# Router logits from the raw residual sums instead of the normalised rows, in a one-core hybrid decoder layer

## The chip, the cores and the metric

The kernel runs as one program on one core of a Trainium2 chip. The metric is the device time of one execution in microseconds (us). Three runs of the kernel before gave 1267.33, 1271.27 and 1271.88 us, median 1271.27 us. The engines of the core are TensorE (PE for its matmuls, PEld for the loads of its stationary operand), VectorE (DVE), ScalarE (ACT), GpSimd (POOL) and SyncE (SP), which issues most of the transfers.

## The reference

One layer of a decoder over 512 rows of 1024 channels. What matters here is the end of the first half and the router of the second half:

```python
def _layer_norm(x, eps=1e-5):
    mu = jnp.mean(xf, axis=-1, keepdims=True)
    var = jnp.mean(jnp.square(xf - mu), axis=-1, keepdims=True)
    return ((xf - mu) * lax.rsqrt(var + eps)).astype(x.dtype)

        y = (1 + g1[:, None]) * (merged @ w_out[l])
        x = _layer_norm(ALPHA * x + y) * ln1_g[l] + ln1_b[l]
        h = _layer_norm(x) * (1 + sc2[:, None]) + sh2[:, None]
        y = (1 + g2[:, None]) * _hier_moe(h, router_grp_w[l], router_grp_b[l], ...)

    # in _hier_moe: 4 groups of 8 experts, one group, two experts inside it
    grp_prob = jax.nn.softmax((x @ w_grp + b_grp).astype(jnp.float32), axis=-1)
    grp_p, grp_idx = lax.top_k(grp_prob, 1)
    exp_logits = (x @ w_exp + b_exp).astype(jnp.float32).reshape(NT, N_GROUPS, EXP_PER_GROUP)
    in_grp = exp_logits[jnp.arange(NT), grp_idx[:, 0]]
    top_l, top_i = lax.top_k(in_grp, TOPK_IN_GROUP)
    comb = grp_p * jax.nn.softmax(top_l, axis=-1)
    # then every expert computes (silu(xb @ w1[e]) * (xb @ w3[e])) @ w2[e] on its rows
```

Each row therefore passes two layer norms in a row (the first with gain and bias `ln1_g`, `ln1_b`) before 36 router logits (4 groups, 32 experts) are taken from it.

## The kernel before

The 512 rows are four tiles (i = 0 to 3) of 128 rows. Three stages matter here.

**The output product.** For each tile, `out_piece` computes `merged @ w_out` as 96 matmuls into `pyo` (128x256 each, three terms of a split into high and low parts), and VectorE adds the residual (`z`, L1105) and gathers statistics (`bn_stats`, L1106). Tiles 0 to 2 are evicted in two pieces of 512 columns, tile 3 in four of 256.

**Norms and routing, the generator `ln`.** For each tile: both norms on VectorE and ScalarE (L1156, L1160, L1161, with the two reciprocal roots on ScalarE, L234 and L235), the normalised rows `xh` (ScalarE L1169, for tile 3 VectorE L1167), eight transposes on TensorE (`ph`, L188) with copies to `h2T`, the split of `xh` into `xhh` (ScalarE L1188) and `xhl` (GpSimd L1189), `acc` (ScalarE L1193), the logits `plg` with the router weights stationary, a copy `lgT` and a second small product that turns them back to rows, then the choice of group and experts on VectorE (L1209 to L1224), a matmul `prk` that counts the rows ahead of each row, and the positions and the one-hot matrix `pm` (L1233 to L1242). At the very end `gather_first` multiplies `xhh` and `xhl` by `pm` (`pgx`, 16 matmuls for a tile), which gathers the rows for the first two experts into `xe`.

**The experts.** All 32 experts' weights (512 KB tiles `ew`, 128x1024) stream from memory over SP's queue through a ring of 36 buffers `Q`, which `z`, `xh`, `acc` and the rest share. The first matmuls of this stage are `p` (L184). SP issues in program order: a transfer whose buffer isn't free holds back everything behind it.

**What sets the order.** The program has one order for each engine, fixed when it is built. A class `Weave` carries a modelled clock, advanced by every matmul (`mm`, `tr`); a generator that yields a number is continued when that clock has moved by so many ns. The constants `LN_D1`, `LN_D2` (the yields of `ln`), and the hand-written calls of `W.upto`, `W.drain` and `gather_first` after the loop over tiles, decide where the norm and routing steps of a tile stand among the products of the next one. On the chip each engine works through its own list in order and waits on semaphores.

Of the kernel before, what the change touches and what calls it, by code (L numbers as in the profile page):

```python
# [67 lines left out]
LN_D1, LN_D2 = 9000, 4500  # L68
# [5 lines left out]
GK = 5  # L74
# [67 lines left out]
def hybrid_kernel(ctx, tc, a, out, dbg=None, stop=None):  # L142
# [836 lines left out]
    sel36 = cp.tile([128, 36], F32, name="sel36")  # L979
    V.tensor_add(sel36, ident[:, 0:36], ident[:, 64:100])  # L980
    l1g = l1b = wr = bfs = None

    def prep():
        nonlocal g1b, l1g, l1b, wr, bfs
# [31 lines left out]
        mm(pbr_[:, 0:36], ones, wsh[:, 288:324], True, True)  # L1016
        V.tensor_add(br, br, pbr_[:, 0:36])
# [106 lines left out]
    gp8, gm, em = rtv[:, 0], rtv[:, 1], rtv[:, 2]  # L1124
    V.memset(gp8, -3e38)
# [4 lines left out]
    lg = pk2[:, 256:384].rearrange("p (i n) -> p i n", i=NT)  # L1130
# [9 lines left out]
    pgx0, stage = [], {i: 0 for i in range(NT)}  # L1140

    def gather_first(tiles, ks=range(8)):


        if not pgx0:
            pgx0.extend(PS("pgx").rearrange("p (k s) -> p k s", k=2) for _ in range(4))
        for k in ks:
            for i in tiles:
                for j, x in enumerate((xhh, xhl)):
                    mm(pgx0[k // 2][:, k % 2, :], x[i][:, k * 128:(k + 1) * 128], hots0[i // 2][:, i % 2, :],  # L1150
                       i == 0 and j == 0 and k % 2 == 0, i == NT - 1 and j == 1 and k % 2 == 1)

    def ln(i, z, st):
        last = i == NT - 1
        mv, rs = layer_stats(z, "l1", st, later=True)
        V.scalar_tensor_tensor(z, z, mv[:, 0:1], l1g, op0=OP.subtract, op1=OP.mult)  # L1156
        st = small("l2st", 12)
        for half in range(2):
            s_ = slice(half * 512, (half + 1) * 512)
            V.scalar_tensor_tensor(z[:, s_], z[:, s_], rs[:, 0:1], l1b[:, s_], op0=OP.mult, op1=OP.add)  # L1160
            V.bn_stats(st[:, half * 6:(half + 1) * 6], z[:, s_])  # L1161
        mv, rs = layer_stats(z, "l2", st, later=last)
        xh = Q("xh")
# [6 lines left out]
        probe(f"x1{i}", z)  # L1170
        probe(f"xh{i}", xh)
        stage[i] = 1
        yield LN_D1
        h2 = []
        for k4 in range(2):
            pt = PS("ph2")
            for k in range(4):
                kk_ = k4 * 4 + k
                tr(pt[:, k * 128:(k + 1) * 128], xh[:, kk_ * 128:(kk_ + 1) * 128], ident)
            t = S("h2T")  # L1180
            if last and k4:
                V.tensor_copy(t, pt)
            else:
                A.activation(t, pt, AF.Copy)
            h2.append(t)
# [17 lines left out]
        lgT = S("lgT")[:, 0:128]
        A.activation(lgT, plg[:, 128:256], AF.Copy)
        stage[i] = 2.5
        yield 700
        mm(plg[:, 0:36], lgT, sel36, True, True)

        V.tensor_add(gp8[:, i, 0:4], plg[:, 0:4], br[:, 0:4])  # L1209
# [362 lines left out]
    for n, u in enumerate(units):  # L1572
# [162 lines left out]
```

## Time and profile before

| quantity | value |
|---|---|
| median of three runs | 1271.27 us (1267.33 to 1271.88) |
| the profiled execution | 1271.63 us, its span 1269.9 us |
| granted TensorE clock, mean of the span | 0.977 of full |
| PE busy | 1176.9 us, 93% of the span |
| DVE busy | 701.2 us, 55% |
| ACT busy | 423.6 us, 33% |
| POOL busy | 121.7 us, 10% |
| moved by SP's transfers (q1) | 268.57 MB |

The profile is one execution. Busy shares are means over stages with different limits, so they don't say what the change is worth; the timeline of each engine around the change does, with the idle time in front of an instruction and what ended it. In a timeline row the first number is the start in us from the start of the span, the second the duration; consecutive instructions of the same kind are joined with a count, and brackets hold the idle time before. PE durations include the pipeline, so the pace of a row of matmuls is the distance between their starts.

### The profile page before, as it was taken

What the parts mean: (1) busy time and instruction counts of PE and PEld (TensorE: products, weight loads), DVE (VectorE), ACT (ScalarE), POOL (GpSimd) and SP (SyncE); (2) the same over time, 40 slices, a digit from 0 to 9 for tenths busy, and PEclk for the clock granted to TensorE, in tenths of its full rate; (3) what the DMA queues carried; (4) which work ended last, traced back from release to release, by engine and by line L of the source; (5) the groups of instructions that cost most, each with busy time, mean ns of one, the idle gap of its engine ahead of it and who ended that gap; (6) DMA issues with size and microseconds to landing.
All of it is one profiled execution on the core that took longest, in us unless ns stands there. A gap on an engine that the chain in (4) does not pass through costs nothing. (4 is left out here: it accounts for less than half of the span.)

```text
span 1269.9 us, 18562 instructions
## 1 busy us (share of the span) xinstructions
PE 1176.9 (93%) x6647; PEld 816.0 (64%) x6647; DVE 701.2 (55%) x1629; ACT 423.6 (33%) x897; POOL 121.7 (10%) x179
## 2 busy tenths in 40 slices
PE   5999999999999999999989969999999899889992
PEld 4788898778888888878778964434435235125352
DVE  5564988777566665323586787535135144133446
ACT  5233666664435364555231321201102002002023
POOL 3011111101101011001150140000000000000002
PEclk9999999999999999999998979999999999999996
DMA  9954413324334243335325197999999999999981
GB/s 325 296 150 141 117 54 118 94 94 133 97 117 120 74 158 108 100 114 183 110 98 183 42 339 295 409 408 409 409 409 409 409 410 406 409 409 407 406 324 67
DMA packets 140862, 297.14 MB, mean 234 GB/s; under 512 B 11099, under 2 KB 82979, under 8 KB 140768
## 3 DMA queue, kind: packets, MB, share of 16 engines
q1 hardware_dynamic: 131296, 268.57, 57.6%
q0 software_dynamic: 8704, 25.00, 6.1%
q10 hardware_dynamic: 768, 2.37, 0.5%
q8 instruction: 53, 0.87, 0.3%
q14 instruction: 41, 0.34, 0.1%
HBM read 293.76 MB, written 4.76 MB: 235 GB/s over the span
## 5 line engine op out<-in xcount | busy, mean ns | idle before, releaser
L184 PE MATMUL p<-ew,xe 128*32 128x512 f32 (+1 forms) x960 | 202.6, 598 | 13.1 <-DMA ew<-in_exp_w_dram 12.7
L277 DVE TENSOR_TENSOR wl<-wst,wh 128x1024 fp32r<-128x1024 f32 (+1 forms) x93 | 119.5, 1314 | 74.7 <-ACT wh L276 74.0
L184 PEld LDWEIGHTS p<-ew,xe 128*32 128x32 f32 (+1 forms) x960 | 53.6, 122 | 155.5 <-issue 81.2
L1473 DVE TENSOR_TENSOR s<-s,p 128x512 f32<-128x512 f32 x13 | 8.9, 688 | 189.9 <-PE p L184 174.2
L184 PE MATMUL py<-ew,aT 128*32 128x512 f32 (+2 forms) x496 | 99.4, 570 | 8.6 <-DMA ew<-in_exp_w_dram 5.8
L276 ACT ACTIVATE wh<-wst 128x1024 fp32r<-128x1024 f32 (+1 forms) x94 | 93.0, 1030 | 27.7 <-POOL wst L275 15.5
L184 PEld LDWEIGHTS py<-ew,aT 128*32 128x32 f32 (+1 forms) x496 | 27.2, 122 | 73.8 <-issue 33.7
L1481 ACT ACTIVATE aT<-pat 128x512 f32<-128x512 f32 x13 | 7.8, 597 | 185.5 <-PE pat L188 185.5
L1522 DVE TENSOR_TENSOR acc<-acc,pcb 128x512 f32<-128x512 f32 x96 | 58.3, 680 | 8.8 <-PE pcb L182 8.8
L1496 ACT ACTIVATE yh<-y 128x512 fp32r<-128x512 f32 (+1 forms) x28 | 16.8, 600 | 136.1 <-DVE y L1494 124.4
L182 PE MATMUL pgx<-pm,xhh 128*128 128x256 f32 (+1 forms) x224 | 58.0, 299 | 1.9 <-DVE pm L1242 1.9
L182 PE MATMUL pgx<-pm,xhl 128*128 128x256 f32 (+1 forms) x224 | 56.3, 291 | 0.0
L515 POOL DMA_DIRECT2D adaw<-in_ada_w_dram x64 | 34.6, 542 | 199.4 <-PE ptp L188 45.5
L1494 DVE SCALAR_TENSOR_TENSOR y<-py,cs,g2b 128x512 f32<-128x512 f32 (+1 forms) x28 | 19.9, 710 | 58.9 <-PE py L184 58.7
L182 PE MATMUL pmg<-hh,wh 128*128 128x512 f32 x128 | 50.4, 394 | 0.0
L182 PE MATMUL psg<-hh,wh 128*128 128x512 f32 x128 | 50.3, 393 | 0.0
L182 PE MATMUL psg<-hl,wh 128*128 128x512 f32 x128 | 49.9, 390 | 0.0
L182 PE MATMUL pmg<-hh,wl 128*128 128x512 f32 x128 | 49.9, 390 | 0.0
L182 PE MATMUL psg<-hh,wl 128*128 128x512 f32 x128 | 49.9, 390 | 0.0
L182 PE MATMUL pmg<-hl,wh 128*128 128x512 f32 x128 | 49.8, 389 | 0.0
L182 PEld LDWEIGHTS pgx<-pm,xhh 128*128 128x128 f32 x224 | 45.0, 201 | 6.3 <-DVE pm L1242 2.3
L182 PE MATMUL pcb<-yh,pT 128*128 128x512 f32 (+1 forms) x112 | 44.3, 399 | 2.2 <-DVEq L1543 2.2
(512 smaller groups left out, 2870.9 us busy)
## 6 DMA issues: line engine op xcount, KB each, us to landing
ew<-in_exp_w_dram SPq DMA_DIRECT2D x380, 512.0 KB, 10.1
wst<-in_w_in_dram SPq DMA_DIRECT2D x66, 512.0 KB, 4.7
adaw<-in_ada_w_dram POOLq DMA_DIRECT2D x64, 256.0 KB, 3.1
adaw<-in_ada_w_dram SPq DMA_DIRECT2D x16, 512.0 KB, 9.2
wst<-in_w_br_hg_dram SPq DMA_DIRECT2D x8, 512.0 KB, 4.0
wst<-in_w_br_nsa_dram SPq DMA_DIRECT2D x8, 512.0 KB, 3.7
wst<-in_w_out_dram SPq DMA_DIRECT2D x8, 512.0 KB, 4.5
ext_d<-ext_d POOLq DMA_DIRECT2D x1, 2560.0 KB, 17.4
```

Source lines behind the costliest of these rows:

```text
L182: PE.matmul(o, l, r, start=start, stop=stop)
L184: PE.matmul(o, l, r, start=start, stop=stop, tile_position=pos)
L276: A.activation(wh, self.w[j], AF.Copy)
L277: (sub or V).tensor_sub(wl, self.w[j], wh.bitcast(F32))
L515: P_.dma_start(w, ada[:, k, 2048 + j * 512:2560 + j * 512])
L1473: V.tensor_mul(s1, s1, p3)
L1481: A.activation(aT, at_.rearrange("p (f s) -> p f s", f=4), AF.Copy)
L1494: V.scalar_tensor_tensor(y, py, cs_, g2b[c0 // 512][:, c0 % 512:c0 % 512 + n], op0=OP.mult, op1=OP.mult)
L1496: A.activation(yh, y, AF.Copy)
L1522: V.tensor_add(acc[i][:, s_], acc[i][:, s_], pc_)
```

## The change

The logits are taken from `z`, the raw sum ahead of both norms. Both norms are affine in a row, so with the weights scaled beforehand by gain and modulation (`rt`, four rows of 36 numbers, made in `prep`) the 36 logits follow from `z @ wr` with the row's two means and two reciprocal roots, in four VectorE instructions on 128x36 (a fifth makes the bias of `xh`). So each tile's `z` is transposed (`pzT`, eight transposes, reading every eighth element of a row), copied to `zT` by ScalarE, and multiplied with `zT` stationary and 36 columns moving (`plg`, eight matmuls); the second small product and its copy `lgT` go. The normalised rows go to `acc` instead of being written over `z`. The generator now has four yields (`LN_T`, `LN_P`, `LN_L`, `LN_R`), tile 3 runs outside of the `Weave` after a full drain, tile 3's `xh` is ScalarE's and its `xhl` VectorE's, all tiles' `pgx` stand together, and the four GpSimd instructions on `g2b` become two VectorE ones later in the program.

```diff
-LN_D1, LN_D2 = 9000, 4500
+LN_T, LN_P, LN_L, LN_R = 1500, 1800, 5500, 4000
...
+        V.tensor_tensor(wsv, wr, col(gc[:, 1, :]), op=OP.mult)
+        total(2, wsv)
+        V.tensor_tensor(wr, wr, col(gc[:, 0, :]), op=OP.mult)
+        total(0, wr)
...
-        mm(pbr_[:, 0:36], ones, wsh[:, 288:324], True, True)
-        V.tensor_add(br, br, pbr_[:, 0:36])
+        mm(pbr_[:, 0:144], ones, wsh[:, 288:432], True, True)
...
+    def z_transposed(i, z, k0, n):
+
+        pt = PS("pzT")[:, 0:128 * n]
+        zv = z.rearrange("p (q k) -> p k q", k=8)
+        for k in range(n):
+            tr(pt[:, k * 128:(k + 1) * 128], zv[:, k0 + k, :], ident)
+        return pt
+
+    def logits_of(i):
+        plg = PS("plg")
+        for k in range(8):
+            mm(plg[:, 0:36], zT[i][k // 4][:, (k % 4) * 128:(k % 4 + 1) * 128], wr[:, k, :], k == 0, k == 7)
+        return plg
...
         mv, rs = layer_stats(z, "l1", st, later=True)
-        V.scalar_tensor_tensor(z, z, mv[:, 0:1], l1g, op0=OP.subtract, op1=OP.mult)
+        ac = Q("acc")
+        acc.append(ac)
+        V.scalar_tensor_tensor(ac, z, mv[:, 0:1], l1g, op0=OP.subtract, op1=OP.mult)
+        if last:
+            plg = tail_logits()
...
+        mv2, rs2 = layer_stats(ac, "l2", st, later=True)
+        if not last:
+            yield LN_T
+            zT[i] = []
+            for k4 in range(2):
+                pt = z_transposed(i, z, k4 * 4, 4)
+                t = S("zT")
+                A.activation(t, pt, AF.Copy)
+                zT[i].append(t)
+            yield LN_P
+            plg = logits_of(i)
+            yield LN_L
+
+        lgi = lg[:, i, 0:36]
+        V.scalar_tensor_tensor(lgi, rt[:, 0], mv[:, 0:1], plg[:, 0:36], op0=OP.mult, op1=OP.add)
+        V.scalar_tensor_tensor(lgi, lgi, rs[:, 0:1], rt[:, 2], op0=OP.mult, op1=OP.add)
+        V.scalar_tensor_tensor(rs2[:, 1:2], mv2[:, 0:1], -1.0, rs2[:, 0:1], op0=OP.mult, op1=OP.mult)
+        V.scalar_tensor_tensor(lgi, rt[:, 1], mv2[:, 0:1], lgi, op0=OP.mult, op1=OP.add)
+        V.scalar_tensor_tensor(lgi, lgi, rs2[:, 0:1], rt[:, 3], op0=OP.mult, op1=OP.add)
+
         xh = Q("xh")
...
+        A.activation(xh.rearrange("p (k q) -> p q k", k=8), ac.rearrange("p (q k) -> p q k", k=8), AF.Identity,
+                     bias=rs2[:, 1:2], scale=rs2[:, 0:1])
         th, tl = Q("xhh", F32R), Q("xhl", F32R)
         A.activation(th, xh, AF.Copy)
-        P_.tensor_sub(tl, xh, th.bitcast(F32))
+        if not last:
+            P_.tensor_sub(tl, xh, th.bitcast(F32))
+        A.activation(ac, ac, AF.Copy, scale=ALPHA)
...
-        stage[i] = 3
-        yield LN_D2
+        if last:
+            gather_first([0, 1, 2])
+        else:
+            yield LN_R
...
+        if last:
+            V.tensor_sub(tl, xh, th.bitcast(F32))
...
-    for q in range(2):
-        P_.tensor_tensor(g2b[q], g2b[q], g2t[q], op=OP.add)
-        P_.tensor_scalar(g2b[q], g2b[q], 1.0, None, op0=OP.add)
-    W.drain(["ln2"])
-    W.upto("ln3", lambda: stage[3] >= 3)
-    gather_first([2], range(GK))
     W.drain()
-    gather_first([2], range(GK, 8))
...
+    for _ in ln(NT - 1, zs[NT - 1], l1st[NT - 1]):
+        pass
```

The change moves instructions on three engines; a piece of each list follows, before and now. (`pk` holds the small tables of the router; its number differs.)

TensorE, inside the output product, around the count `prk` of tile 0, before:

```order
L182 MATMUL pyo<-wl,mh 128x256
L182 MATMUL pyo<-wh,ml 128x256
L182 LDWEIGHTS pk_5855
L182 MATMUL prk<-pk_5855 128x32
L182 MATMUL pyo<-wh,mh 128x256
L182 MATMUL pyo<-wl,mh 128x256
L182 MATMUL pyo<-wh,ml 128x256
```

and now, with the eight logit matmuls of tile 1 behind it:

```order
L181 MATMUL pyo<-wl,mh 128x256
L181 MATMUL pyo<-wh,ml 128x256
L181 LDWEIGHTS pk_5856
L181 MATMUL prk<-pk_5856 128x32
L181 MATMUL plg<-pk_5856,zT 128x36 x8
L181 MATMUL pyo<-wh,mh 128x256
L181 MATMUL pyo<-wl,mh 128x256
```

The logits of tile 1 now wait behind the same `prk`, in the middle of the product; before, they stood apart from it as two smaller pieces.

ScalarE, from the second norm's root of one tile to the copies of the transposed rows, before (tile 2; `h2T` are the copies of its own transposed rows):

```order
L234 ACTIVATE l2rs<-l2mv,eps 128x1
L235 ACTIVATE l2rs<-l2rs 128x1
L1169 ACTIVATE xh<-z,l2rs 128x128x8
L1184 ACTIVATE h2T<-ph_7100 128x512
L1184 ACTIVATE h2T<-ph_7107 128x512
L1188 ACTIVATE xhh<-xh 128x1024
L1193 ACTIVATE acc<-z 128x1024
L234 ACTIVATE l1rs<-l1mv,eps 128x1
L235 ACTIVATE l1rs<-l1rs 128x1
```

and now (tile 0's `xh`, `xhh` and `acc`, then `zT` of tile 1):

```order
L233 ACTIVATE l2rs<-l2mv,eps 128x1
L234 ACTIVATE l2rs<-l2rs 128x1
L1223 ACTIVATE xh<-acc,l2rs 128x128x8
L1226 ACTIVATE xhh<-xh 128x1024
L1229 ACTIVATE acc<-acc 128x1024
L1209 ACTIVATE zT<-pzT 128x512 x2
```

What a logit product needs (`zT`) now stands behind the `xh`, `xhh` and `acc` of the tile ahead of it.

VectorE, from the last eviction of the output product on, before (statistics of tile 3 directly behind the last `bn_stats`):

```order
L1105 SCALAR_TENSOR_TENSOR z<-z,pyo 128x256
L1106 BN_STATS l1st<-z 128x6
L232 BN_AGGR l1mv<-l1st 128x2
L1156 SCALAR_TENSOR_TENSOR z<-z,l1mv,l1g 128x1024
L1160 SCALAR_TENSOR_TENSOR z<-z,l1rs,l1b 128x512
L1161 BN_STATS l2st<-z 128x6
L1160 SCALAR_TENSOR_TENSOR z<-z,l1rs,l1b 128x512
L1161 BN_STATS l2st<-z 128x6
```

and now (the logits of tile 2 behind that `bn_stats`, followed by its routing and positions):

```order
L1121 SCALAR_TENSOR_TENSOR z<-z,pyo 128x256
L1122 BN_STATS l1st<-z 128x6
L1216 SCALAR_TENSOR_TENSOR pk_6594<-wsh,l1mv,plg 128x36
L1217 SCALAR_TENSOR_TENSOR pk_6594<-pk_6594,l1rs,wsh 128x36
L1218 SCALAR_TENSOR_TENSOR l2rs<-l2mv,l2rs 128x1
L1219 SCALAR_TENSOR_TENSOR pk_6594<-wsh,l2mv,pk_6594 128x36
L1220 SCALAR_TENSOR_TENSOR pk_6594<-pk_6594,l2rs,wsh 128x36
L1233 MAX pk_6593<-pk_6594 128x8
```

The statistics of tile 3 (`l1mv`) moved behind all of tile 2's routing and positions; their place in the list is shown here:

```order
L1257 TENSOR_TENSOR t_7178<-pk_6594,prk 128x64
L1258 TENSOR_REDUCE pos<-t_7178 128x2
L1261 TENSOR_SCALAR lk<-pos 128x2
L1262 SCALAR_TENSOR_TENSOR lk<-ef,pos 128x2
L1263 TENSOR_TENSOR lk<-lk 128x2
L1265 TENSOR_SCALAR te_7184<-cst,lk 128x256
L1266 SCALAR_TENSOR_TENSOR pm<-cst,lk,te_7184 128x256
L231 BN_AGGR l1mv<-l1st 128x2
L1194 SCALAR_TENSOR_TENSOR acc<-z,l1mv,l1g 128x1024
L1200 SCALAR_TENSOR_TENSOR acc<-acc,l1rs,l1b 128x512
```

So nothing of tile 3's norms is ahead of `pm` of tile 2 on VectorE.

## Rows read from the trace of the kernel before

**Rows 1.** Windows of the span: start and end in us, length, then busy time and instruction count of PE, PEld, DVE, ACT, POOL, the granted TensorE clock (1.00 is full), the busy share of the transfer engines and GB/s.

```profile
760.00:765.00 5.00, 4.53 (x21) 4.23 (x21) 2.53 (x10) 1.02 (x2) 0.00 (x0) 0.50 0.01 3
...
850.00:1000.00 150.00, 142.14 (x693) 62.88 (x693) 54.61 (x127) 19.55 (x39) 0.00 (x0) 1.00 1.03 409
1150.00:1210.00 60.00, 58.58 (x270) 25.15 (x269) 22.41 (x46) 6.79 (x15) 0.00 (x0) 1.00 1.02 407
```

**Rows 2.** The waits of SP's transfer queue between 690 and 860 us: what it waited for, us in total, times, longest.

```profile
SPq L1270 <- PE p L184: 22.9, 12, 15.4
```

**Rows 3.** The timeline of PE in the output product.

```profile
718.78 0.19 PE L182 MATMUL prk<-pk 128*128 128x32 bf16 x1 [0.58 <-DVE pk L1223]
...
721.77 1.04 PE L188 MATMUL ph<-cst,xh 128*128 128x128 f32 x8
722.57 0.36 PE L182 MATMUL pyo<-wh,mh 128*128 128x256 f32 x1
...
724.17 1.09 PE L184 MATMUL plg<-h2T,pk 128*64 128x128 f32 x16
725.19 0.39 PE L182 MATMUL pyo<-wh,mh 128*128 128x256 f32 x1
...
733.46 0.18 PE L182 MATMUL prk<-pk 128*128 128x32 bf16 x1 [0.57 <-DVE pk L1223]
```

**Rows 4.** The timeline of the weight loads (PEld): the transposes and the second small logit product in the output product, and four transposes of `s` in the expert stage that read every fourth element.

```profile
721.67 0.90 PEld L188 LDWEIGHTS ph<-cst,xh 128*128 128x128 f32 x8
...
726.60 0.31 PEld L182 LDWEIGHTS plg<-sel,lgT 128*128 128x128 f32 x2
726.83 0.19 PEld L182 LDWEIGHTS pyo<-wh,mh 128*128 128x128 f32 x1
...
781.09 0.56 PEld L188 LDWEIGHTS pat<-cst,s 128*128 128x128 f32 x4 [1.77 <-DVE s L1473]
```

**Rows 5.** The timeline of DVE around tile 1's eviction, its two norms and the routing of tile 0, and the first and last step of the positions of tile 1.

```profile
707.30 0.69 DVE L1105 SCALAR_TENSOR_TENSOR z<-z,pyo 128x512 f32<-128x512 f32 x1 [3.23 <-PE pyo L182]
...
709.00 1.28 DVE L1156 SCALAR_TENSOR_TENSOR z<-z,l1mv,l1g 128x1024 f32<-128x1024 f32 x1
...
713.72 0.73 DVE L1160 SCALAR_TENSOR_TENSOR z<-z,l1rs,l1b 128x512 f32<-128x512 f32 x1
...
715.22 0.21 DVE L232 BATCH_NORM_AGGREGATE l2mv<-l2st 128x2 f32<-128x12 f32 x1
...
716.29 0.17 DVE L1210 MAX8 pk<-pk 128x8 f32<-128x8 f32 x1
...
718.47 0.25 DVE L1223 SCALAR_TENSOR_TENSOR pk<-cst,ef,pk 128x32 bf16<-128x32 f32 x1
...
735.04 0.20 DVE L1233 TENSOR_TENSOR t<-pk,prk 128x64 f32<-128x64 f32 x1
...
736.39 0.48 DVE L1242 SCALAR_TENSOR_TENSOR pm<-cst,lk,te 128x256 fp32r<-128x256 f32 x1
```

**Rows 6.** The timeline of ACT beside it: `xh`, one copy out of PSUM, `xhh`, `acc` and the first step of a root.

```profile
708.23 0.59 ACT L1184 ACTIVATE h2T<-ph 128x512 f32<-128x512 f32 x1
...
716.22 2.22 ACT L1169 ACTIVATE xh<-z,l2rs 128x1024 f32<-128x1024 f32 x1 [0.23 <-DVE l2rs L237]
...
723.38 1.06 ACT L1188 ACTIVATE xhh<-xh 128x1024 fp32r<-128x1024 f32 x1
724.33 1.06 ACT L1193 ACTIVATE acc<-z 128x1024 f32<-128x1024 f32 x1
...
725.48 0.29 ACT L234 ACTIVATE l1rs<-l1mv,eps 128x1 f32<-128x1 f32 x1
```

**Rows 7.** The timeline of PE from the last matmul of the output product to the first of the experts.

```profile
736.32 0.28 PE L182 MATMUL pyo<-wh,ml 128*128 128x256 f32 x1
...
746.01 0.52 PE L182 MATMUL plg<-sel,lgT 128*128 128x36 f32 x2 [3.12 <-ACT lgT L1204]
...
757.37 0.58 PE L182 MATMUL pgx<-pm,xhh 128*128 128x256 f32 x1 [1.42 <-DVE pm L1242]
...
765.88 3.16 PE L184 MATMUL p<-ew,xe 128*64 128x512 f32 x12
```

**Rows 8.** The timeline of all engines at 749.5 us: one VectorE instruction and the GpSimd instruction beside it.

```profile
749.53 2.41 DVE L1223 SCALAR_TENSOR_TENSOR pk<-cst,ef,pk 128x32 bf16<-128x32 f32 x1
749.56 2.34 POOL L1189 TENSOR_TENSOR xhl<-xh,xhh 128x1024 fp32r<-128x1024 f32 x1 [5.09 <-ACT xhh L1188]
```

**Rows 9.** The timeline of PE earlier in the output product, two waits for the merged rows.

```profile
682.12 0.39 PE L182 MATMUL pyo<-wh,mh 128*128 128x256 f32 x1 [1.18 <-ACT mh L1071]
...
684.89 0.58 PE L182 MATMUL pyo<-wh,mh 128*128 128x256 f32 x1 [1.66 <-ACT mh L1071]
```

**Rows 10.** Windows as in rows 1, cut at the moments at which the granted clock changed.

```profile
684.70:688.20 3.50, 3.31 (x14) 3.08 (x15) 0.69 (x1) 0.14 (x1) 0.00 (x0) 0.51 0.82 283
...
742.80:746.20 3.40, 0.28 (x3) 0.19 (x2) 2.70 (x6) 0.66 (x3) 1.66 (x4) 1.00 1.06 395
...
757.30:766.70 9.40, 8.85 (x42) 7.81 (x44) 5.91 (x27) 2.04 (x4) 0.23 (x1) 0.50 0.11 45
```

**Rows 11.** The timeline of DVE where the router's weights are prepared (the first row is one of the reductions; of the second the idle time in front is the point).

```profile
597.67 0.68 DVE L1007 TENSOR_REDUCE wsh<-wsh 128x36 f32<-128x288 f32 x1
...
603.91 0.19 DVE L1017 TENSOR_TENSOR br<-br,pbr__5997 128x36 f32<-128x36 f32 x1 [4.29 <-PE pbr__5997 L182]
```

More of the change, by code (lines that the diff above doesn't have):

```diff
@@ L978, in hybrid_kernel @@
     br = cp.tile([128, 36], F32, name="br")
-    sel36 = cp.tile([128, 36], F32, name="sel36")
-    V.tensor_add(sel36, ident[:, 0:36], ident[:, 64:100])
-    l1g = l1b = wr = bfs = None
+    l1g = l1b = wr = bfs = rt = None
     def prep():
-        nonlocal g1b, l1g, l1b, wr, bfs
+        nonlocal g1b, l1g, l1b, wr, bfs, rt
         g1b = row_bc("g1b", mod_d[0:1, 0:1024])
@@ L1138, in hybrid_kernel @@
     hots0 = [S("pm", F32R).rearrange("p (i s) -> p i s", i=2) for _ in range(2)]
-    pgx0, stage = [], {i: 0 for i in range(NT)}
+    pgx0 = []
     def gather_first(tiles, ks=range(8)):
@@ L1146, in gather_first @@
             pgx0.extend(PS("pgx").rearrange("p (k s) -> p k s", k=2) for _ in range(4))
[L1147 to L1151, printed above, removed]
+        end = tiles[-1] == NT - 1
+        for part in ((xhh,), (xhl,)) if end else ((xhh, xhl),):
+            for k in ks:
+                for i in tiles:
+                    for x in part:
+                        mm(pgx0[k // 2][:, k % 2, :], x[i][:, k * 128:(k + 1) * 128], hots0[i // 2][:, i % 2, :],
+                           i == 0 and x is xhh and k % 2 == 0, end and x is xhl and k % 2 == 1)
+    zT = {}
+    def z_transposed(i, z, k0, n):
[9 more added lines that the diff above has]
+        return plg
     def ln(i, z, st):
@@ L1170, in ln @@
[L1170 to L1185, printed above, removed]
+            V.scalar_tensor_tensor(ac[:, s_], ac[:, s_], rs[:, 0:1], l1b[:, s_], op0=OP.mult, op1=OP.add)
@@ L1203, in ln @@
[L1203 to L1209, printed above, removed]
         V.max(gm[:, i, :], gp8[:, i, :])
         V.max_index(gi[:, i, :], gm[:, i, :], gp8[:, i, :])
-        V.tensor_add(lg[:, i, :], plg[:, 4:36], br[:, 4:36])
         gif = rtv[:, 3, i, 0:1]
@@ L1217, in ln @@
                         op0=OP.not_equal, op1=OP.mult)
[L1218 removed]
+        V.tensor_add(elc[:, i, :], elc[:, i, :], lg[:, i, 0:32])
         V.max(em[:, i, :], elc[:, i, :])
@@ L1292, in hybrid_kernel, with tail_logits @@
         P_.dma_start(g2t[q], a["ada_b"][0:1, 5120 + q * 512:5632 + q * 512].to_broadcast([128, 512]))
-    W.upto("ln2", lambda: stage[2] >= 2)
-    W.upto("ln3", lambda: stage[3] >= 1)
-    W.upto("ln2", lambda: stage[2] >= 2.5)
-    W.drain(["ln0", "ln1"])
-    gather_first([0, 1])
-    W.upto("ln2", lambda: stage[2] >= 3)
-    W.upto("ln3", lambda: stage[3] >= 2)
-    for q in range(2):
-        P_.tensor_tensor(g2b[q], g2b[q], g2t[q], op=OP.add)
-        P_.tensor_scalar(g2b[q], g2b[q], 1.0, None, op0=OP.add)
-    W.drain(["ln2"])
-    W.upto("ln3", lambda: stage[3] >= 3)
-    gather_first([2], range(GK))
-    W.drain()
-    gather_first([2], range(GK, 8))
+    W.drain()
+    def tail_logits():
+        i = NT - 1
+        zT[i] = []
+        for k4 in range(2):
+            pt = z_transposed(i, zs[i], k4 * 4, 4)
+            t = S("zT")
+            A.activation(t, pt, AF.Copy)
+            zT[i].append(t)
+        return logits_of(i)
+    for _ in ln(NT - 1, zs[NT - 1], l1st[NT - 1]):
+        pass
     load_unit((0, 1), 8, 12, w_first)
@@ L1608, in to_come @@
                 place_experts(srt)
+                for q in range(2):
+                    V.scalar_tensor_tensor(g2b[q], g2b[q], 1.0, g2t[q], op0=OP.add, op1=OP.add)
             if nxt:
```

64 lines of the change are left out of this document (29 added, 35 removed).

## The prediction

> **What bounds the kernel now.** I read the windows first, because the busy shares of the whole span mix three stages. In the expert stage the transfer engines are busy all the time: the share is 1.03 at 409 GB/s between 850 and 1000 us and still 1.02 between 1150 and 1210 [rows 1]. No faster computation shortens that stage; it can only begin earlier or later. Just ahead of it stands the one stretch in which the transfers stop: 0.01 busy, 3 GB/s, from 760 to 765 [rows 1]. The waits of SP's queue name the reason: it stood 15.4 us at a stretch until a `p`, the first expert product, gave its weight buffers back [rows 2]. All of the ring that could be filled ahead had been filled. So the end of the program stands at a fixed distance from the first `p`, at 765.88 [rows 7], and the question is what the change does to that start.
>
> The second view is PE's timeline ahead of it. The last matmul of the output product starts at 736.32 and leaves PE 0.12 later; I call that moment T = 736.44. From T to `p` there are 29.44 us [rows 7], in which PE waits for the routing of tiles 2 and 3. Before T, PE is nearly always busy: the waits among the products of tiles 1 to 3 are 0.58 and 0.57 [rows 3]. Whatever is added to PE before T, or makes it wait there, moves T; whatever shortens the chain from T to `p` is gained.
>
> **The change: PE's work before T.** Before, two of the four sets of logits lie in front of T. A set is 0.80 for the transposes (721.77 to 722.57), 1.02 for the sixteen narrow matmuls (724.17 to 725.19) [rows 3] and 0.23 for the second small product (its loads start at 726.60, the next one's at 726.83) [rows 4]: 2.05, twice 4.10. Now three sets lie there. The nearest row for the new logit matmul is that second product: also 36 columns in full precision with a 128x128 stationary, 0.23. Eight make 1.84; the lower end is the old set's 1.02 for eight products. The transposes read every eighth element. Bounds: 0.80 as before, and 1.12 by the four loads that read every fourth element, 0.56 [rows 4], twice; I take 0.94. A set is 2.78, three 8.34: **+4.2 us** (from +1.4 to +4.8).
>
> The Trainium skill, "SBUF — State Buffer", section "Door 1: The DMA port swizzle", says that single precision can be strided by up to four elements for free and that each access to a new 16-byte line pays a penalty. That speaks against transposes at a stride of eight. The trace has 0.14 per load at a stride of four against 0.11 for contiguous ones (0.90 for eight) [rows 4]; at the penalty of the former the sum would rise by 0.5.
>
> **The change: new waits before T.** In the product of tile 2, PE now has 36 matmuls, 8 transposes and 24 matmuls from the end of tile 1's product to `prk` of tile 0: 60 x 0.12 + 0.94 = 8.1 us. VectorE has more to do in that time, since tile 0's logits stand behind tile 1's second norm. By the rows of tile 1 [rows 5], counted from the last matmul's end at 707.1: the piece, its statistics and their sum to 709.0; the first norm's instruction 1.3; two halves of 1.5 each (the half from 713.72 ends at 715.22); 0.25 for the sum; the five new small instructions, about 0.22 each by the spacing of small ones between 716.29 and 718.47, 1.1; routing to `pk` 2.3 (716.29 to 718.72, less one instruction that is gone). That is 9.9: PE waits 1.8. Behind `prk` stand the logits of tile 1. They need `zT`, which ScalarE copies behind tile 0's `xh`, `xhh` and `acc`. `xh` can begin when the third of the five has run, 7.3 after the product's end; then 2.2, 0.95, 0.95 and a copy of 0.6 [rows 6]: 12.0. PE waits another 2.1. Queued behind it is the rest of tile 2's product, so everything moves. Together 3.9 with the gaps between instructions, 3.2 by the durations alone; I take 3.6. Tile 2's product has the same list for tiles 1 and 2, so twice: 7.2, less the 1.15 that went: **+6.0 us**. Were the copies and the routing early after all, it would be -1.15, the lower end.
>
> **The granted clock before T.** After waits of 1.18 and 1.66 us close together [rows 9] the granted clock was 0.51 in the next 3.5 us, where 14 matmuls ran in 3.31 us [rows 10], 0.236 each against 0.12: 1.6 us lost. The new pairs of waits are as long. I count one and a half such dips: **+2.4 us** (0 to 4.8, three dips).
>
> **From T to `p`.** New order, at full clock, counted from the new T. Last piece and statistics on VectorE to 1.1; logits and routing of tile 2, which stand behind them, to 4.5; `prk`, then positions. These start at 5.0, as GpSimd starts `xhl` of tile 2 (VectorE's small instruction at 749.53 took 2.41 beside such an `xhl`, which took 2.34 [rows 8]; alone it takes 0.25 [rows 5]). So `pm` of tile 2 is ready at 9.0 instead of 6.9 (the seven steps are 1.83 from 735.04 on [rows 5]). Then tile 3's statistics and root, 0.3 and 0.5, and a copy 0.6: its logits run from 10.4 to 12.2. Next are 48 `pgx` at 0.12, to 18.0. VectorE meanwhile does the first norm to 10.6, the halves to 13.6, logits and routing to 17.4, so `prk` follows the `pgx`; positions to 20.0; `xhl` of tile 3, now VectorE's, about 1.25 (as the first norm's instruction of the same size) to 21.2; eight `pgx` and the count to 22.5, `p` at 22.8. Against 29.44: **-6.6 us**. What is gained here: tile 2's positions no longer run beside GpSimd's work on `g2b`, and tile 3's logits need one product instead of two with a copy between. What is given back: the 32 `pgx` of tiles 0 and 1, which ran while VectorE was busy, are on the path now (32 x 0.12 = 3.8). The `g2b` steps return as two VectorE instructions of half the size of the first norm's, 1.3 together, in the expert stage, where VectorE is busy for 54.61 of 150 us [rows 1]: no cost, and 1.3 if nothing hid them.
>
> The clock again: PE stands nearly idle from T to T+10.4. Before, with PE 0.28 busy of 3.40 us to 746.2, the level was half in all of 757.3 to 766.7, although PE was busy for 8.85 of these 9.40 us [rows 10]. There 42 instructions took 0.21 each. At that pace the 48 `pgx` take 10.1 and the logits 3.2 instead of 5.8 and 1.8: at most +5.7, and 0 if the level doesn't fall. I take **+2.8 us**, half of it, since the work is in one piece. The first `p` ran at half level from 765.88 to 766.7 before, and will run at full: **-0.4**.
>
> **The rest.** Three more reductions (0.68 each) and two products of the same size or less on VectorE in `prep` are at most 3.4 us, beside an idle of 4.29 us in front of the row that needs them [rows 11]: 0, and 3.4 if that idle weren't there. SP's order is the same; one of the four weight buffers that were free before the first `p` now comes free only with tile 3's `xhl`, some 1.5 us ahead of `p`, when the queue stands idle anyway: 0, up to 1.3 (512 KB at 409 GB/s).
>
> **Sum.** 4.2 + 6.0 + 2.4 - 6.6 + 2.8 - 0.4 = +8.4 on the profiled execution's 1271.63 us, which lies 0.36 above the median: **1280.0 us**. 0.5%, 6.4 us, is about what a measurement tells from no change; slower then means above 1277.6.
>
> **Rivals.** *The new waits don't come* (not slower). If `zT` and the routing of the tile ahead arrive in time, 7.2 of waits and 2.4 of clock go: 1270.4. For it speaks that the waits rest on a sum of VectorE durations that exceeds PE's by 1.8 only; against it that the logits, too, stand behind four ScalarE instructions, 2.1 more. It decides from the point at which tile 0's `xh` could start 4 us sooner; faster than 1264.9 needs the tail's half clock gone besides.
>
> *The half level stays* through the tail and takes three dips before T: 2.8 becomes 5.7 and 2.4 becomes 4.8, 1285.3. For it: it held through 9.4 us of nearly unbroken matmuls before. Against: PE's work in the tail is now in one piece.
>
> *The logits are cheap*: their loads overlap. At 1.02 a set instead of 1.84, in four places, 3.3 less: 1276.7. Against it is the 0.23 row; for it, that this row starts from a single product. The Trainium skill, "TensorE: Matmul & The Clock Gate", section "Back-to-back issue gap", gives about 81 ns for a load and matmul in a stream at 128 columns; an estimate by that page is 1.3 for the sixteen pairs of a set, and the sum would be 2.2 lower.
>
> *The start of `p` doesn't set the end*: no change, 1271.3. Against it is the transfer share at its ceiling for 400 us.
>
> That the third tile's routing runs inside the last product isn't a gain to be waited for: only its logit product does. VectorE's list has the routing behind the last eviction.
>
> **Chances.** Forecast 0.60 (its own range 1274 to 1286; slower 0.46, same 0.14), no new waits 0.18 (same 0.10, faster 0.08), half level 0.10 (slower), cheap logits 0.06 (same 0.04, slower 0.02), fixed end 0.06 (same). Slower 0.58, same 0.34, faster 0.08. Eight in ten lie from 1269 to 1286.
>
> **What would show it.** In the new timeline of PE: eight `plg` in 1.8 us; idle time in front of the `prk` of tiles 0 and 1 on VectorE's `pk`, 1.8, and in front of the `plg` behind them on `zT`, 2.1; the last matmul of the product some 12.6 later than 736.3; `p` 22 to 26 us after that; a granted clock of 0.5 for a while behind the waits. It is wrong if these waits are under 1 us, or if the transfers run at less than 1.02 in the expert stage.

## The result and the profile after

The changed kernel takes 1283.74 us (median of four runs, 1282.37 to 1283.93); the kernel before, 1270.83 us in the runs beside it. The ratio is 1.0098 with a 95% interval of 1.0085 to 1.0112: slower by 12.9 us. The profiled execution has a span of 1282.0 us against 1269.9.

The timeline of TensorE in the output product after the change (start, duration, and in brackets the idle time before and its end):

```profile
699.20 1.07 PE L187 MATMUL pzT<-cst,z 128*128 128x128 f32 x8
...
702.98 1.87 PE L181 MATMUL plg<-pk,zT 128*128 128x36 f32 x16
...
718.98 0.18 PE L181 MATMUL prk<-pk 128*128 128x32 bf16 x1 [1.65 <-DVE pk L1245]
720.73 3.33 PE L181 MATMUL plg<-pk,zT 128*128 128x36 f32 x16 [1.57 <-ACT zT L1209]
723.86 0.56 PE L181 MATMUL pyo<-wh,mh 128*128 128x256 f32 x1
```
These rows answer to [rows 3]. A logit set at full clock is 0.82 for the transposes and 1.70 for the logits (702.98 to the next product at 704.68). In front of `prk` and of the logits behind it TensorE now waits 1.65 and 1.57 us, where it waited 0.58; the logits then take 3.13 (720.73 to 723.86), almost twice as long as those at 702.98. The same view from the second pair of waits to the first expert product, which answers to [rows 7]:

```profile
739.93 0.18 PE L181 MATMUL prk<-pk 128*128 128x32 bf16 x1 [1.61 <-DVE pk L1245]
741.68 3.63 PE L181 MATMUL plg<-pk,zT 128*128 128x36 f32 x16 [1.57 <-ACT zT L1209]
...
750.82 0.28 PE L181 MATMUL pyo<-wh,ml 128*128 128x256 f32 x1
...
755.56 0.19 PE L181 MATMUL prk<-pk 128*128 128x32 bf16 x1 [4.40 <-DVE pk L1245]
...
760.74 3.63 PE L181 MATMUL plg<-pk,zT 128*128 128x36 f32 x16 [3.21 <-ACT zT L1329]
764.17 0.56 PE L181 MATMUL pgx<-pm,xhh 128*128 128x256 f32 x1
...
774.37 1.18 PE L181 MATMUL pgx<-pm,xhh 128*128 128x256 f32 x8 [2.05 <-DVE pm L1266]
...
777.34 1.12 PE L183 MATMUL p<-ew,xe 128*64 128x512 f32 x2
```
The pair of waits comes again at 739.93, and the logits behind it take 3.44 (to the next product at 745.12). The last product starts at 750.82 instead of 736.32, and `p` at 777.34 instead of 765.88: 14.5 us later and 11.5 us later. The windows (length, busy time and count of PE, PEld, DVE, ACT, POOL, then the granted clock, the transfer share, GB/s) answer to [rows 1, 10]:

```profile
703.00:704.70 1.70, 1.70 (x19) 1.70 (x17) 0.15 (x1) 0.00 (x0) 0.00 (x0) 1.00 0.68 253
717.00:720.70 3.70, 0.51 (x4) 0.23 (x3) 3.39 (x14) 3.67 (x5) 1.38 (x1) 1.00 0.00 0
720.70:728.00 7.30, 7.28 (x36) 7.28 (x36) 2.03 (x6) 0.46 (x1) 0.98 (x1) 0.53 0.00 0
...
741.60:748.40 6.80, 6.72 (x31) 6.72 (x32) 2.44 (x8) 0.51 (x2) 2.72 (x4) 0.50 0.73 273
...
760.70:768.90 8.20, 8.16 (x38) 8.17 (x39) 6.64 (x24) 4.78 (x6) 0.00 (x0) 0.50 0.82 314
...
772.40:775.40 3.00, 1.03 (x8) 1.01 (x8) 2.79 (x8) 0.00 (x0) 0.00 (x0) 1.00 0.00 0
775.40:778.90 3.50, 3.50 (x18) 2.32 (x18) 2.23 (x8) 2.33 (x7) 0.00 (x0) 0.54 0.48 150
850.00:1000.00 150.00, 142.68 (x706) 66.73 (x706) 60.49 (x136) 20.28 (x40) 0.00 (x0) 1.00 1.03 409
```
At 703 the logits run at full clock. From 717.0 to 720.7 TensorE is busy for 0.51 of 3.70 us, and the mean clock of the 7.3 us behind it is 0.53, which is half the full clock for about 6.8 of them; the second pair is followed by 6.8 us at 0.50. In the tail it is half again to 768.9 and once more from 775.4, behind the wait for `pm`. The transfers stand at 0.00 from 772.4 to 775.4, as they stood before `p` in the kernel before, and at 1.03 in the expert stage, as ever. What SP's queue waited for behind the output product (total, times, longest):

```profile
SPq L1296 <- DVE xhl L1268: 11.7, 1, 11.7
...
SPq L1296 <- PE p L183: 9.8, 11, 4.4
```
Its longest stand behind the output product is now for `xhl` of tile 3 (11.7 us), which gives back the last buffer that can be filled ahead, and then for `p`, as in [rows 2]. Last, VectorE beside GpSimd in the tail:

```profile
755.91 2.35 POOL L1228 TENSOR_TENSOR xhl<-xh,xhh 128x1024 fp32r<-128x1024 f32 x1 [6.63 <-ACT xhh L1226]
...
756.29 2.00 DVE L1261 TENSOR_SCALAR lk<-pos 128x2 f32<-128x2 f32 x1
...
772.89 0.17 DVE L1261 TENSOR_SCALAR lk<-pos 128x2 f32<-128x2 f32 x1
```
The third small step of tile 2's positions takes 2.00 beside `xhl`, as [rows 8] had it; the same step of tile 3, with GpSimd idle, takes 0.17.

### The profile page after: what moved, and what is told of

The parts are those of the page before. It is cut to its first block, busy times and chain, and to the rows that moved or that the text cites. A ratio compares the mean times of both kernels' runs of the same rounds, so it can differ in the third digit from the quotient of the medians.

```text
span 1282.0 us, 18552 instructions
## 1 busy us (share of the span) xinstructions
PE 1182.2 (92%) x6639; PEld 821.8 (64%) x6639; DVE 703.3 (55%) x1643; ACT 424.9 (33%) x895; POOL 113.2 (9%) x176
## 5 line engine op out<-in xcount | busy, mean ns | idle before, releaser
L276 DVE TENSOR_TENSOR wl<-wst,wh 128x1024 fp32r<-128x1024 f32 (+1 forms) x93 | 124.2, 1364 | 74.9 <-ACT wh L275 73.9
```

The source lines that it names most:

```text
L276: (sub or V).tensor_sub(wl, self.w[j], wh.bitcast(F32))
```

## The experiments

All kernels but the last three of this section were timed in three rounds against the kernel before on the same chip; the ratios are to its time in those rounds (medians 1271.07, 1271.22 and 1270.39 us), while the table's first row is that of the result.

| kernel | median, us | ratio to before, 95% interval | last product | `p` | span minus `p` |
|---|---|---|---|---|---|
| before (profiled) | 1270.83 | 1 | 736.32 | 765.88 | 504.0 |
| changed | 1283.74 | 1.0098 (1.0085 to 1.0112) | 750.82 | 777.34 | 504.7 |
| early_logits | 1268.59 | 0.9980 (0.9969 to 0.9990) | 737.28 | 761.01 | 504.6 |
| zt_first | 1280.16 | 1.0064 (1.0045 to 1.0083) | 747.13 | 773.64 | 504.7 |
| filled_waits | 1282.62 | 1.0096 (1.0079 to 1.0112) | 749.10 | 775.49 | 503.5 |
| before_g2b | 1268.37 | 0.9986 (0.9976 to 0.9997) | 735.30 | 761.13 | 503.0 |
| gather_ahead | 1279.63 | 1.0070 (1.0048 to 1.0092) | 751.25 | 774.15 | 503.4 |
| tail_filled | 1287.42 | 1.0120 (1.0091 to 1.0150) | 752.91 | 782.26 | 503.9 |
| tail_filled_half | 1281.00 | 1.0089 (1.0066 to 1.0111) | 751.60 | 774.29 | 504.6 |
| best_a | 1263.37 | 0.9937 (0.9915 to 0.9959) | 737.79 | 755.93 | 503.8 |
| best_b | 1264.38 | 0.9952 (0.9936 to 0.9969) | 737.72 | 757.52 | 504.6 |

The last column is the check on the first step of the prediction: `p` moves over 26 us in these eleven traces, and the rest of the program behind it stays within 1.7 us (503.0 to 504.7).

**early_logits: the new waits away.**

```diff
-LN_T, LN_P, LN_L, LN_R = 1500, 1800, 5500, 4000
+LN_T, LN_P, LN_L, LN_R = 1500, 1800, 3000, 4000
```

> The changed kernel with the yield LN_L at 3000 instead of 5500: each tile's logits and routing stand on VectorE ahead of the next tile's last eviction, and its xh, xhh and acc on ScalarE ahead of the next tile's zT. Theory (the new waits and the half clock behind them are the loss): the four waits of 1.57 to 1.65 us on pk and zT go, the logit products run at 1.70 instead of 3.13 and 3.44, so the last product ends 6.4 + 6.1 us sooner; the tail is about 2.3 shorter since the third tile's routing is partly inside. Against the changed kernel about -14 us, near 1269, at or below the kernel before. Rival (the logit products themselves, three sets of 2.5 and the 48 pgx on the path, are the loss): not below 1277.

Measured 1268.59, the 1269 that the theory gave, from one constant of the program; the kernel before took 1271.07 in the same rounds. The waits of TensorE from 690 to 765 us:

```profile
PE plg L181 <- ACT zT L1329: 3.6, 1, 3.6
PE pgx L181 <- DVE pm L1266: 2.0, 1, 2.0
PE prk L181 <- DVE pk L1245: 1.5, 1, 1.5
```
All of them lie behind the last product, which starts at 737.28. The four of the changed kernel are gone, and the three logit sets ahead of it run at full clock (only that of tile 3, at 744.38, runs at half). The rival falls: the logit products and the 48 `pgx` are all still there.

**zt_first: one wait of each pair away.** ScalarE copies `zT` ahead of the other tile's `xh`.

```diff
         else:
             yield LN_R
+            xh = Q("xh")
+            A.activation(xh.rearrange("p (k q) -> p q k", k=8), ac.rearrange("p (q k) -> p q k", k=8), AF.Identity,
+                         bias=rs2[:, 1:2], scale=rs2[:, 0:1])
...
+            A.activation(ac, ac, AF.Copy, scale=ALPHA)
```

> The changed kernel with xh, xhh, xhl and acc of a tile written behind the yield LN_R, so that ScalarE copies zT of the next tile ahead of them; VectorE's order is as it was. Both theories: the two waits on zT (3.1 us) go, the two on pk (1.65 and 1.61) stay. If the clock falls only behind the pair of waits, the half clock before the last product ends goes too: about -9, 1274.5. If one wait of 1.6 is enough for it to fall: about -3 to -5, 1279 to 1281.

Measured 3.6 us below the changed kernel, so the second reading. The timeline of TensorE and the windows at the first wait:

```profile
720.38 0.18 PE L181 MATMUL prk<-pk 128*128 128x32 bf16 x1 [1.65 <-DVE pk L1247]
720.41 2.72 PE L181 MATMUL plg<-pk,zT 128*128 128x36 f32 x16
```
```profile
720.40:721.60 1.20, 1.20 (x11) 1.20 (x11) 1.17 (x3) 1.17 (x3) 0.01 (x1) 0.91 0.00 0
721.60:728.20 6.60, 6.60 (x32) 6.60 (x32) 3.38 (x8) 0.86 (x1) 2.36 (x1) 0.50 0.00 0
...
741.90:745.20 3.30, 3.30 (x18) 3.30 (x17) 3.13 (x7) 0.00 (x0) 2.97 (x5) 0.50 0.79 305
```
The wait on `zT` is gone: the logits start with `prk`. But here the 1.65 us on `pk` are enough: about 1 us later the clock falls, to 0.50 for at least 6.6 us, and behind the second such wait (1.61) for 3.3 us, although the logits stand behind that one just the same.

**filled_waits: the waits stay, TensorE works through them.**

```diff
+    def fill(n):
+        for _ in range(n):
+            PE.matmul(prk[:, 256:512], ones, iota, start=True, stop=True)
...
+        if 0 < i < NT - 1:
+            fill(4)
         plg = PS("plg")
...
+        if i < 2:
+            fill(4)
         o = prk[:, i * 32:(i + 1) * 32]
```

> The changed kernel with four matmuls on constants (256 columns in full precision, into columns of prk that nothing reads) ahead of each of the prk of tiles 0 and 1 and ahead of the logits of tiles 1 and 2, where TensorE waits. The waits' length stays, but TensorE works through them. Theory (the idle time lets the clock fall): granted clock 1.00 there, logit products of 1.70 instead of 3.13 and 3.44, 6.1 us less, about 1277.5. Rival (the clock falls because of the narrow logit matmuls): the half level stays, 1283.7 or up to 1 us more.

The timeline of TensorE there:

```profile
720.01 0.18 PE L181 MATMUL prk<-pk 128*128 128x32 bf16 x1
721.60 1.99 PE L1185 MATMUL prk<-cst,ones 128*128 128x256 f32 x8 [1.42 <-DVE t L1265]
723.43 1.87 PE L181 MATMUL plg<-pk,zT 128*128 128x36 f32 x16
...
741.28 1.99 PE L1185 MATMUL prk<-cst,ones 128*128 128x256 f32 x8 [1.67 <-DVE t L1265]
```
```profile
714.00:751.00 37.00, 32.35 (x246) 30.80 (x246) 24.25 (x78) 11.82 (x17) 6.90 (x6) 1.00 0.44 150
```
The logits at 723.43 take 1.71, and the clock is full throughout, so the narrow matmuls alone don't lower it. Idle time is part of what does, but its length alone doesn't settle it: a wait of 1.67 us is left here, ahead of wide matmuls, and the clock stays, where one of 1.65 right ahead of the logits was enough in zt_first. The time did not follow: 1282.62. The added matmuls write to a tile that VectorE still reads, so they wait 1.42 and 1.67 themselves and then take 1.8. From the transposes to the logits it is 9.01 and 9.26 us instead of 7.33 and 7.33, 3.6 of the 6.1 that the clock gave back; the last product ends 2.7 sooner, counted from the same place. That filling the waits keeps the clock up is shown, the price of the half level there only by the difference.

**before_g2b: one part of the change alone, in the kernel before.**

```diff
-    for q in range(2):
-        P_.tensor_tensor(g2b[q], g2b[q], g2t[q], op=OP.add)
-        P_.tensor_scalar(g2b[q], g2b[q], 1.0, None, op0=OP.add)
...
                 place_experts(srt)
+                for q in range(2):
+                    V.scalar_tensor_tensor(g2b[q], g2b[q], 1.0, g2t[q], op0=OP.add, op1=OP.add)
```

> The kernel before with one part of the change alone: the four GpSimd instructions on g2b become two VectorE ones in the expert stage. Theory (VectorE stands still beside them in the positions of tile 2, 2.2 us more than the same steps take elsewhere, and 1.1 us in the routing before it, both on the chain to p): -3 us, 1268. Rival (another wait ends last there): no change, 1271.

Measured 2.7 us faster. VectorE in tile 2's positions, in the kernel before:

```profile
754.78 1.20 DVE L1239 TENSOR_TENSOR lk<-lk 128x2 f32<-128x2 f32 x1
...
756.83 0.48 DVE L1242 SCALAR_TENSOR_TENSOR pm<-cst,lk,te 128x256 fp32r<-128x256 f32 x1
```

and without GpSimd's work on `g2b` beside them:

```profile
752.34 0.16 DVE L1239 TENSOR_TENSOR lk<-lk 128x2 f32<-128x2 f32 x1
...
752.93 0.48 DVE L1242 SCALAR_TENSOR_TENSOR pm<-cst,lk,te 128x256 fp32r<-128x256 f32 x1
```
From the last product to `p` it is 25.7 instead of 29.4 us; this step of the positions takes 0.16 instead of 1.20, and `pm` starts 0.59 behind its start instead of 2.05. So this part of the change gains by itself, and the rest of it, in its place, lost some 15 us. It also means that early_logits, at 1268.59, gains no more than this part gives alone: by these two medians, taking the logits from `z` brought nothing of its own there.

**gather_ahead, tail_filled and tail_filled_half: the tail.** gather_ahead moves the 32 `pgx` of tiles 0 and 1 up; the other two leave the order as it is and put matmuls on constants into the two waits.

```diff
-            gather_first([0, 1, 2])
+            gather_first([2])
...
+    gather_first([0, 1])
     for _ in ln(NT - 1, zs[NT - 1], l1st[NT - 1]):
```

> The changed kernel with the 32 pgx of tiles 0 and 1 written right behind the output product, ahead of tile 2's prk and tile 3's logits, and only tile 2's 16 behind those. If the pgx on the path set the tail: TensorE's row of 48 pgx, which ended at 772.06, shrinks to 16, prk follows VectorE's routing at about 768, so p comes about 4 us sooner: 1279 to 1280. If VectorE's chain set the tail, as the forecast had it at full clock (17.4 against 18.0): under 1 us.

> The changed kernel with 18 matmuls on constants (256 columns, full precision, into unread columns of prk) behind the output product and 16 ahead of tile 3's logits, where TensorE waits for VectorE; nothing else moves. If the half clock in the tail is what the 48 pgx lose: granted clock 1.00, logits 1.70 instead of 3.43, all pgx at 0.12, p about 3.5 us sooner, 1280. If the half clock there costs nothing since VectorE is later anyway: no change, 1283.7.

> As tail_filled, with 9 and 7 matmuls instead of 18 and 16, since one took 0.43 us there: 3.9 and 3.0 us, which fits into the waits of 4.4 and 3.2. If the half clock in the tail is what the 48 pgx lose: full clock, logits 1.70, pgx at 0.12, p about 3.5 us sooner than in the changed kernel, 1280. If VectorE is later anyway: 1283.7.

gather_ahead gave 4.1 us, as its first reading had it: `prk` follows VectorE's routing at 768.41. But the order isn't the only thing that it changes, since the clock came back too (its logits take 1.8 us instead of 3.43); from the last product to `p` it is 22.8 us. tail_filled was a miss: I had counted 0.21 us for such a matmul, and it takes 0.43, so the filling itself delayed `prk` and the logits. With half as many, TensorE's timeline and clock read:

```profile
756.34 0.18 PE L181 MATMUL prk<-pk 128*128 128x32 bf16 x1 [0.54 <-DVE pk L1245]
...
761.56 1.98 PE L181 MATMUL plg<-pk,zT 128*128 128x36 f32 x16 [1.03 <-ACT zT L1334]
...
769.21 0.27 PE L181 MATMUL prk<-pk 128*128 128x32 bf16 x4
...
774.29 1.98 PE L183 MATMUL p<-ew,xe 128*64 128x512 f32 x4
```
```profile
751.70:773.00 21.30, 17.69 (x124) 16.16 (x123) 18.13 (x60) 10.38 (x12) 2.35 (x1) 1.00 0.75 276
```
The logits start at 761.56 and take 1.7, the 48 `pgx` end at 769.21, and from the last product to `p` it is 22.6 us instead of 26.4. Nothing but constants was added, so 3.8 us of the tail are the price of the half level there, in these two traces. All 48 `pgx` are still in their place, and the tail is as short as in gather_ahead: they cost 4 us on the path because they ran at half level. The median fell by 2.7 only; single runs of one kernel differ by up to 7 us (the kernel before, 1268.40 to 1275.58), and in this trace the last product ends 0.8 later.

**best_a and best_b: a version that beats both.** LN_L is 500 and 3000; further:

```diff
-            plg = tail_logits()
+            tail_T()
+            gather_first([1])
...
+        if last:
+            W.drain()
+            plg = logits_of(i)
...
-            gather_first([0, 1, 2])
+            gather_first([2])
...
-    W.drain()
+    gather_first([0])
     for _ in ln(NT - 1, zs[NT - 1], l1st[NT - 1]):
```

> The changed kernel with three things at once: LN_L 500 (each tile's logits ahead of the next tile's last evictions), the pgx of tile 0 and of tile 1 around tile 3's transposes, and the third tile's count and positions behind tile 3's second statistics instead of ahead of its first. Theory: no new waits before the product's end (it ends as in early_logits, near 737.4), TensorE busy through most of the tail, so full clock, and VectorE's chain from there 1.1 + 0.25 + 1.3 + 3.0 + 0.25 + 1.85 + 1.1 + 2.4 + 1.85 + 1.25 = 14.4 and some 2 us of GpSimd's block: p at 738 + 17, about 755 instead of 761.0 in early_logits: 1262 to 1264, below both kernels. Rival (the start of p no longer sets the end, or the half clock stays): not below 1267.

> As best_a with LN_L 3000, so that the third tile's logits stand behind three of the four last evictions instead of two. By the same sums VectorE reaches tile 3's statistics 1.4 us later: 1.4 us above best_a, if VectorE's chain sets the tail there; equal if something else does.

best_a takes 1263.37, 7.9 us below the kernel before in the same rounds and 20 below the changed one; best_b is 1.0 above it (`p` 1.6 later), where 1.4 were expected. The windows of best_a:

```profile
735.00:740.00 5.00, 5.00 (x44) 5.00 (x43) 4.55 (x19) 4.19 (x5) 2.15 (x1) 1.00 1.02 408
740.00:745.00 5.00, 4.70 (x43) 4.54 (x42) 4.71 (x9) 1.47 (x4) 2.35 (x5) 1.00 1.00 345
745.00:750.00 5.00, 3.68 (x18) 3.59 (x19) 4.40 (x23) 3.26 (x3) 0.00 (x0) 0.54 1.02 373
750.00:755.00 5.00, 2.95 (x18) 2.87 (x18) 2.82 (x8) 1.26 (x3) 0.00 (x0) 0.50 1.03 410
```
TensorE stays at full clock until 745 and then falls to half level, so the full clock that the theory wanted for most of the tail did not come; the time came out as forecast all the same. The transfer share is 1.00 to 1.03 in all windows up to 755: the queue now fills its free buffers nearly up to `p` at 755.93. With this gap closed, a still earlier `p` might bring less; that was not tried.

**late_plg, wide_wait_short and wide_wait_long: how long the half level lasts.** One execution each. They start from zt_first and move the logits behind wide products.

```diff
-LN_T, LN_P, LN_L, LN_R = 1500, 1800, 5500, 4000
+LN_T, LN_P, LN_L, LN_R = 1500, 5600, 1700, 4000
```

with 2700 and 1400 in the last place for the other two.

> zt_first with the logit product 36 matmuls later (LN_P 5600, LN_L 1700), so that after the wait of prk on pk (1.65 us) the wide products of pyo follow at once and the narrow logits stand 4.3 us behind them. In zt_first the half level began some 1.3 us after that wait and lasted about 6.7 us. If the narrow logits behind the wait are what keeps it down so long: half for about 3.5 us here, as after the waits between 681 and 685 in the kernel before, or not at all. If any work follows the same course: about 6.7 us again. The time itself also changes by the later routing of tile 2 and is not to be compared.

> late_plg with LN_R 2700: prk of tiles 0 and 1 stands 12 matmuls of the product earlier, so that TensorE waits about 1.4 us there on pk, and 48 wide products follow at once, the logits 5.8 us behind. If a wait of that size ahead of wide products lowers the clock: half level for 3 to 7 us in pyo from about 1 us behind it. If the clock falls only where the narrow logits follow (as in zt_first, 1.65 us): granted clock 1.00 throughout, and the last product ends about 2.8 us later than in late_plg by the waits alone.

> late_plg with LN_R 1400: prk stands directly behind the transposes, 24 matmuls earlier, the wait on pk about 2.9 us, then 60 wide products. As long as the pair of waits in the changed kernel (3.2 us). If the kind of work behind the wait decides how long the half level lasts: about 3.5 us of half level, against 7.3 and 6.8 in the changed kernel. If not: about 7 us again.

late_plg missed its question: the wait on `pk` disappeared (1269.26 us, beside 1271.29 of the kernel before), because the 1.70 us of tile 0's logits now lie on TensorE between the end of tile 1's product and that `prk`, where it waited 1.65. The other two (1272.39 and 1280.28 us, beside 1269.82) have waits of 1.31 and 2.74 us ahead of wide products. Windows of wide_wait_short behind its wait, and of wide_wait_long:

```profile
717.50:720.00 2.50, 2.46 (x21) 2.46 (x22) 2.23 (x7) 2.10 (x3) 1.25 (x1) 1.00 0.00 0
720.00:723.00 3.00, 3.00 (x27) 3.00 (x27) 2.93 (x4) 0.00 (x0) 1.16 (x1) 1.00 0.00 0
```

and

```profile
720.30:723.60 3.30, 3.30 (x17) 3.30 (x17) 3.23 (x4) 0.45 (x1) 1.97 (x1) 0.50 0.00 0
723.60:727.00 3.40, 3.40 (x30) 3.40 (x29) 0.67 (x1) 0.00 (x0) 0.00 (x0) 0.99 0.00 0
...
737.30:740.70 3.40, 3.30 (x16) 3.30 (x16) 3.30 (x7) 2.14 (x3) 2.05 (x1) 0.50 1.01 371
740.70:744.00 3.30, 3.30 (x30) 3.30 (x29) 2.68 (x9) 0.00 (x0) 0.93 (x3) 0.99 0.95 387
```
The short wait leaves the clock at 1.00. Behind the long ones it is half for 3.3 and 3.4 us and full again in the next window. In the changed kernel the level stayed down for about 6.8 us both times behind waits of 3.2 us, and there the narrow logits were the first work behind the wait. That the kind of work decides the length is not shown, though, and two traces speak against it. Early in the output product, zt_first has the two waits of [rows 9] again (1.16 and 1.60 us on `mh`), with nothing but wide products behind them:

```profile
684.15 0.58 PE L181 MATMUL pyo<-wh,mh 128*128 128x256 f32 x1 [1.60 <-ACT mh L1087]
```
```profile
683.80:690.70 6.90, 6.55 (x29) 6.33 (x30) 0.77 (x2) 0.30 (x1) 0.00 (x0) 0.51 0.81 304
```
There the half level lasts 6.9 us, against 3.5 in the kernel before [rows 10]. And gather_ahead has the same instructions as the changed kernel up to the last product, but its first stretch lasts 10.3 us (0.50 from 719.0 to 729.3). So about the same waits with the same work behind them gave different lengths, and what decides the length is open.

## Why the prediction was right, and which size was off

The direction, the place and the mechanism came out as forecast: slower, by waits of TensorE inside the output product that outweigh a shorter tail. The time, 1283.74 against 1280.0, lies in the range of 1274 to 1286, and nearer to the rival with the longer half level (1285.3). Term by term, on the profiled executions:

| term | forecast, us | measured, us | from |
|---|---|---|---|
| logit sets ahead of the last product | +4.2 | +3.5 | 3 x 2.52 - 4.10 |
| new waits | +6.0 | +5.2 | 1.65 + 1.57 + 1.61 + 1.57 - 1.15 |
| granted clock there | +2.4 | +6.2 | logits 1.43 + 1.74 longer, the products behind them 1.7 and 1.3 |
| tail at full clock | -6.6 | -6.9 | 22.57 in tail_filled_half - 29.44 |
| clock in the tail | +2.8 | +3.8 | 26.40 - 22.57 |
| `p` at full clock | -0.4 | in the rest | half level once more from 775.4 |
| start of the stretch and rest | 0 | -0.3 | `p` moved by 11.5 |

**The step that failed in size is the granted clock before the last product.** The prediction took it from the one dip in [rows 10], 3.5 us and 1.6 us lost, and counted one and a half of them. One dip was too little to take a price from: wide_wait_long has two of 3.3 and 3.4 us, but the waits of [rows 9] came again in zt_first with 6.9 us behind them. In the place that counts, behind both pairs of waits the level stayed down twice as long, about 6.8 us, and the logits, which lie in it, took twice their time. Two dips of 3.1 us lost each stand where one and a half of 1.6 were counted; even the rival's three dips (4.8) were too little. What decides the length is open. The terms sum to 8.4 in the forecast and to 11.5 in the traces: of the 3.1 between them this term makes 3.8 and the clock in the tail 1.0, while the logit sets (-0.7) and the waits (-0.8) went the other way, which is luck. The medians differ by 12.9: 0.6 of the rest lies behind `p`, and 0.8 is how far the profiled executions lie from the medians.

**The waits.** The sum of VectorE's rows gave 1.8 for `pk`, measured 1.65 and 1.61; ScalarE's gave 2.1 for `zT`, measured 1.57. A pair is 3.2, which is the sum of the durations alone; the 3.6 that I took was 0.4 too high. early_logits shows that they and the clock behind them are the loss: it keeps every instruction and ends the product at 737.28.

**The logit sets.** Eight logits are 1.70, by the 0.23 row 1.84. The cheap logits of the rival (1.02) fall. So does the lower estimate from the Trainium skill, "TensorE: Matmul & The Clock Gate", section "Back-to-back issue gap": 1.3 for the sixteen load-and-matmul pairs, measured 1.70.

**The transposes.** I took 0.94 for a stride of eight elements, measured 0.82, against 0.80 for contiguous rows. The rule of the Trainium skill, "SBUF — State Buffer", section "Door 1: The DMA port swizzle", that single precision strided by more than four elements pays a penalty, does not show in the pace of these transposes; the measurement decides. The 0.14 for a load at a stride of four in [rows 4] was a misreading: 0.56 is the length of a row of four with the whole of the last load in it, and the next loads start at 781.56, 0.47 behind the first, which is 0.12 a load.

**The tail.** 22.8 was worked out for full clock, 22.57 measured once TensorE was kept busy; in the changed kernel it was 26.4, just past the 22 to 26 that the prediction named. `pm` of tile 2 came 8.5 us after the product's end, behind the 2.00 us of GpSimd's block (forecast 9.0), `plg` at 9.8 (10.4). Keeping the work in one piece did not bring the clock back sooner, as I had assumed in halving 5.7: a run of `pgx` at half level ended at 768.9.

**Rests.** The prepared tables cost nothing that shows; SP started seven weight transfers between 754.3 and 763.6, then stood 11.7 us for `xhl`, and started the eighth at 775.39, with the end at the same distance from `p` (504.7 us against 504.0). The rival of a fixed end falls by the last column of the table.

## What to carry to other kernels

A new product on an engine that bounds its stage should be placed by what feeds it, not by where the old one stood: by one yield the changed kernel was 13 us slower or 2.5 faster than the kernel before, and 7.9 faster with the tail's order changed as well. Where a stage ends at a wait of the transfers, find the last thing that gives buffers back, and price every edit by that moment. Price a wait of TensorE with the clock behind it, and give that price a range: one dip in one execution doesn't tell how long the next one lasts.

## What the runs showed that was not expected

The length of the half level is not fixed by the waits and the work around it: 3.5 us in the kernel before [rows 10] and 6.9 in zt_first behind the same pair of waits on `mh` with the same wide products, 6.8 in the changed kernel and 10.3 in gather_ahead behind the same waits with the same logits. And a fall can come late: in zt_first TensorE had worked for about 1 us again before the level fell behind a wait of 1.65 us, while waits of 1.31 us (wide_wait_short) and 1.67 us (filled_waits) ahead of wide products left it alone.
